# S5 scan with the backward direction in reversed time, its input matrices prepared for all groups, and one step of the cosine on ScalarE

## Chip, cores and metric

One core of a Trainium2 chip runs the whole program. The metric is the device time of one execution in microseconds. The kernel before was run three times: median 1742.31 us, lowest 1741.55, highest 1746.58. In the text, PE is TensorE, DVE VectorE, ACT ScalarE, POOL GpSimd and SP the engine whose queue issues nearly all DMAs. Everything is computed in float32 (some products in a split of it).

## What is computed

The reference is one encoder block on 1024 positions of 1024 channels. The change lies in one of its two token mixers, S5: 512 channels in 32 groups of 16, each group with 64 complex states per direction. Cut to that:

```python
def _s5_scan(u, lam_re, lam_im, log_step, b_re, b_im, c_re, c_im, reverse):
    step = exp(log_step)[:, None]; mag = exp(lam_re * step)
    abar_re, abar_im = mag * cos(lam_im * step), mag * sin(lam_im * step)
    # coef = (abar - 1) / lam, complex
    bb_re = coef_re[..., None] * b_re - coef_im[..., None] * b_im
    bb_im = coef_re[..., None] * b_im + coef_im[..., None] * b_re
    bu_re = einsum('blgc,gpc->lbgp', ug, bb_re); bu_im = einsum('blgc,gpc->lbgp', ug, bb_im)
    # state(t) = abar * state(t-1) + bu(t); from the end where reverse
    s_re, s_im = associative_scan(combine, (a_re, a_im, bu_re, bu_im), reverse=reverse)
    return einsum('lbgp,gcp->blgc', s_re, c_re) - einsum('lbgp,gcp->blgc', s_im, c_im)

y = u * d + _s5_scan(u, ..., reverse=False) + _s5_scan(u, ..., reverse=True)
z = gelu(y); y_a = (z * sigmoid(z @ glu_w + glu_b)) @ w_branch_a
```

The other mixer (Hyena: projections, short convolutions and long convolutions in the frequency domain), the gates, the merge and a SwiGLU feed-forward layer follow.

## The kernel before

The block is emitted stage by stage (hybrid_block, line 1780): norm and Hyena filters, four projections with convolutions, S5 (emit_s5, line 738), eight more projections with convolutions, the gates' projections (emit_gates_a), the GLU on S5's result (emit_glu), Hyena, the merge, the feed-forward layer. A scheduler of the framework sets the order on each engine from the stages' order as written and a model of the engines; on the chip each engine then takes its instructions in that fixed order. So TensorE's projections of the later stages stand between the S5 products, and GpSimd's remainders of the weights (wl, line 136, in the split of a float32 weight into two parts) between its S5 work.

S5 has 128 partitions: 0 to 63 hold the forward direction's 64 states, 64 to 127 the backward direction's (f and b in the code). Time is cut into 128 chunks of 8 steps. s5_params (line 595) computes the per-state coefficients as small [128, 32] arrays, on VectorE; its pool is given back when they are done, and only then are the loop's first loads issued. The loop over q (line 772) takes four of the 32 groups at a time:

- It loads b and c of the four groups (braw, craw), multiplies b by the coefficient on GpSimd (cmul, lines 591 and 592, with tiles bt, giving Bb), and with the powers of abar in a chunk (wt, giving Bw), also on GpSimd.
- c with the powers gives CC on VectorE (lines 797, 798). TensorE transposes c (tc, line 786) and Bw (tt, line 807); ScalarE copies the latter to BT.
- kp (line 819) gives the kernel inside a chunk, which goes through DRAM to a Toeplitz matrix D.
- The phase of each chunk's rotation (lines 839 to 843, ACT and DVE) becomes sine and cosine: three passes on ScalarE (lines 845 to 847: the absolute value and two sines), a square on ScalarE (848), 1 - 2x on VectorE (849), a product on VectorE (850).
- bu, the chunks' inputs to the states, is eight products on TensorE (line 856), 128 x 128 with 128 columns, for real and imaginary parts of four groups. VectorE rotates it (860 to 862) into xs.
- VectorE scans xs over the chunks, once forwards on partitions 0 to 63 and once backwards in the free dimension on 64 to 127, each for the real and the imaginary part (S):

```python
V.tensor_tensor_scan(out=o[f, 1:n], data0=r[f, 0:n - 1], data1=x[f, 0:n - 1], ...)
V.tensor_tensor_scan(out=o[b, n - 2::-1], data0=r[b, n - 1:0:-1], data1=x[b, n - 1:0:-1], ...)
```

- The states are rotated back into M, the real part on VectorE and the imaginary part on GpSimd (875 to 877, tiles rt and beside). TensorE sums C times M over both directions and D times the input in yp (881, 883), 12 products. ScalarE copies yp to z (885), which goes to DRAM (zS).

Tiles with one buffer (z, S, ph, M) and the engines' fixed orders set what can run ahead. In PSUM, bu0, bu1 and yp have a bank each.

Of the kernel before, what the change touches and what calls it, by code (L numbers as in the profile page):

```python
# [7 lines left out]
F32 = mybir.dt.float32  # L8
# [41 lines left out]
def make_constants():  # L50
# [57 lines left out]
    for s_ in range(2):  # L108
# [12 lines left out]
        "c_j8": np.repeat(np.stack([8.0 * np.arange(P), 8.0 * np.arange(P)[::-1]]).astype(np.float32), 64, axis=0),  # L121
# [473 lines left out]
def s5_params(E, op, sp, ps):  # L595
# [136 lines left out]
    keep = op.tile([P, 5, G], F32, name="s5keep")  # L732
    for i, a in enumerate((cre, cim, r8, w, wl)):
        nc.gpsimd.tensor_copy(keep[:, i], a)
    return (keep[:, 0], keep[:, 1]), keep[:, 2], keep[:, 3], keep[:, 4], ec, eb


def emit_s5(E, before):
# [5 lines left out]
    with ExitStack() as ctx:  # L744
# [7 lines left out]
        with E.tc.tile_pool(name="s5p", bufs=1, reuse_waits="tile") as pp:  # L752
            coef, r8, wh, wl, ec, eb = s5_params(E, op, pp, ps)
            before()
# [17 lines left out]
        for q in range(8):  # L772
            gs = slice(4 * q, 4 * q + 4)
            B4 = lambda ap, n: ap[:, gs].unsqueeze(2).to_broadcast([P, 4, n])
            braw = [T(f"braw{i}", [P, 4, 16], 2) for i in range(2)]
            craw = [T(f"craw{i}", [64, P], 2) for i in range(2)]
            for s in range(2):
                r = slice(64 * s, 64 * s + 64)
                for i, n in enumerate(("re", "im")):
                    nc.sync.dma_start(out=braw[i][r], in_=d["s5_b_" + n][0, s, gs].rearrange("g p c -> p g c"))  # L780
# [18 lines left out]
            Bb = [T(f"bb{i}", [P, 4, 16], 2) for i in range(2)]  # L799
            cmul(E, sp, Bb, braw, [B4(coef[0], 16), B4(coef[1], 16)], [P, 4, 16], "bt", GP)  # L800
# [48 lines left out]
            V.tensor_scalar(out=co, in0=co, scalar1=-2.0, scalar2=1.0, op0=ALU.mult, op1=ALU.add)  # L849
# [3 lines left out]
            for i in range(2):  # L853
                pt = ps.tile([P, 4, P], F32, tag=f"bu{i}", name=f"bu{i}")
                for g in range(4):
                    nc.tensor.matmul(out=pt[:, g], lhsT=BT[i][:, g], rhs=U[:, g], start=True, stop=True)
                bu.append(pt)
# [8 lines left out]
            for i in range(2):  # L866
                o, r, x = fl(S[i]), fl(rd), fl(xs[i])
                V.tensor_tensor_scan(out=o[f, 1:n], data0=r[f, 0:n - 1], data1=x[f, 0:n - 1], initial=0.0,
                                     op0=ALU.mult, op1=ALU.add)
                V.tensor_tensor_scan(out=o[b, n - 2::-1], data0=r[b, n - 1:0:-1], data1=x[b, n - 1:0:-1], initial=0.0,  # L870
# [7 lines left out]
            yp = ps.tile([P, 4, P], F32, tag="yp", name="yp")  # L878
            for g in range(4):
                for k in range(2):  # L880
# [1028 lines left out]
```

## Time and profile before

| | |
|---|---|
| median of three runs | 1742.31 us (1741.55 to 1746.58) |
| profiled execution, its own time | 1741.92 us |
| its span | 1740.1 us |
| PE busy | 1548.8 us (89%) |
| PEld (weight loads) busy | 1282.4 us (74%) |
| DVE busy | 1352.2 us (78%) |
| ACT busy | 720.0 us (41%) |
| POOL busy | 674.4 us (39%) |
| S5 loop | about 400 to 634 us of the span |

The span runs from the first to the last instruction of the program; the execution's own time also has what lies around it. The profile's shares are means over stages with different limits, so a stage has to be looked at by itself: its windows, its groups of instructions, its waits. An instruction's names are those of its tiles (out<-in); a matmul in float32 appears as two records.

### The profile page before, as it was taken

The numbers are of one execution on the slowest core, as the hardware profiler recorded it, in microseconds if no ns is written. First come the engines' busy times: TensorE is split into PE (matmuls) and PEld (weight loads), VectorE is DVE, ScalarE is ACT, GpSimd is POOL, SyncE is SP. The second block draws the span as 40 slices with busy tenths as digits, with TensorE's granted clock in tenths as the row PEclk, the third lists the DMA queues.
The fourth block names the chain that finished last, engine by engine and source line by source line (L and its number), as shares of the span: only waits on it lengthen the run. The fifth ranks groups of instructions, "written<-read, shape, count | busy, mean of one in ns | idle before, by whom it ended". The sixth has DMA issues, their size and how long they took to land. (4 is left out here: it accounts for less than half of the span.)

```text
span 1740.1 us, 21907 instructions
## 1 busy us (share of the span) xinstructions
PE 1548.8 (89%) x7470; PEld 1282.4 (74%) x7470; DVE 1352.2 (78%) x1945; ACT 720.0 (41%) x1326; POOL 674.4 (39%) x475
## 2 busy tenths in 40 slices
PE   6777889998777798998869999899999999999996
PEld 2666768776666676786757989688888888878884
DVE  6889798688999935788887666976676777579976
ACT  5846455543333325412223355533333333245445
POOL 3356654329775526768862121111111111011242
PEclk9999999998888899999979999899999999999998
DMA  9446643423232235874326753143323223499963
GB/s 330 122 140 185 194 120 111 154 77 102 64 78 58 76 98 168 292 236 146 120 85 208 258 176 97 49 137 112 103 91 103 91 97 103 147 374 312 331 193 124
DMA packets 245318, 263.81 MB, mean 152 GB/s; under 512 B 28120, under 2 KB 169264, under 8 KB 243765
## 3 DMA queue, kind: packets, MB, share of 16 engines
q1 hardware_dynamic: 244726, 259.99, 47.0%
q0 software_dynamic: 480, 2.42, 0.4%
q8 instruction: 59, 0.97, 0.2%
q14 instruction: 53, 0.43, 0.1%
HBM read 195.00 MB, written 67.34 MB: 151 GB/s over the span
## 5 line engine op out<-in xcount | busy, mean ns | idle before, releaser
L144 PE MATMUL pj<-hT,wh 128*128 128x512 f32 x480 | 196.0, 408 | 10.0 <-ACT cva L1180 8.9
L146 PE MATMUL pj<-hT,wl 128*128 128x512 f32 x480 | 194.5, 405 | 3.5 <-POOL wl L136 3.5
L136 POOL TENSOR_TENSOR wl<-wf,wh 128x1024 fp32r<-128x1024 f32 (+1 forms) x56 | 130.5, 2330 | 157.6 <-ACT wh L135 129.8
L136 POOL TENSOR_TENSOR wl<-wg,wh 128x1024 fp32r<-128x1024 f32 x22 | 54.7, 2488 | 346.9 <-ACT wh L135 346.8
L146 PE MATMUL gu<-h2T,op 128*128 128x512 f32 x440 | 173.1, 394 | 4.3 <-DVE op L136 4.3
L144 PE MATMUL gu<-h2T,op 128*128 128x512 f32 x440 | 171.4, 394 | 2.6 <-ACT op L135 2.5
L145 PE MATMUL gu<-h2T,op 128*128 128x512 f32 x440 | 172.7, 392 | 0.0
L135 ACT CAST op<-ws 128x512 fp32r<-128x512 f32 x88 | 54.4, 621 | 181.3 <-PE gu L146 109.4
L145 PE MATMUL dn<-dop 128*128 128x512 f32 x308 | 120.1, 390 | 0.4 <-POOL dop L136 0.4
L146 PE MATMUL dn<-dop 128*128 128x512 f32 x308 | 119.9, 389 | 0.0
L144 PEld LDWEIGHTS pj<-hT,wh 128*128 128x128 f32 x480 | 94.5, 197 | 29.5 <-ACT cva L1180 9.6
L144 PE MATMUL dn<-dop 128*128 128x512 f32 x308 | 112.4, 390 | 2.9 <-ACT dop L135 2.9
L146 PEld LDWEIGHTS pj<-hT,wl 128*128 128x128 f32 x480 | 93.9, 196 | 23.1 <-POOL wl L136 4.3
L145 PE MATMUL pj<-hT,wh 128*128 128x512 f32 x256 | 104.6, 409 | 0.0
L146 PEld LDWEIGHTS gu<-h2T,op 128*128 128x128 f32 x440 | 83.6, 190 | 22.7 <-DVE op L136 5.2
L144 PEld LDWEIGHTS gu<-h2T,op 128*128 128x128 f32 x440 | 83.7, 190 | 21.3 <-ACT op L135 3.4
L145 PEld LDWEIGHTS gu<-h2T,op 128*128 128x128 f32 x440 | 83.7, 190 | 17.2
L145 PE MATMUL pj<-lT,wh 128*128 128x512 f32 x224 | 89.8, 401 | 0.0
L136 POOL TENSOR_TENSOR dop<-bf,dop 128x512 fp32r<-128x512 f32 x17 | 32.2, 1897 | 128.8 <-ACT dop L135 112.5
L1531 DVE TENSOR_TENSOR ws<-wu 128x512 f32<-128x512 f32 x22 | 24.9, 1130 | 66.2 <-DMA wu<-in_ffn_w_gu_dram 66.2
L144 PE MATMUL wop<-woh,mT 128*128 128x256 f32 x256 | 73.1, 286 | 2.3 <-DVE tmp L1406 2.1
L145 PE MATMUL wop<-wol,mT 128*128 128x256 f32 x256 | 72.5, 283 | 0.0
(458 smaller groups left out, 4503.5 us busy)
## 6 DMA issues: line engine op xcount, KB each, us to landing
bf<-in_ffn_w_down_dram SPq DMA_DIRECT2D x105, 256.0 KB
wf<-in_w_in_dram SPq DMA_DIRECT2D x36, 512.0 KB
ada<-in_ada_w_dram SPq DMA_DIRECT2D x48, 256.0 KB
wg<-in_ffn_w_gu_dram SPq DMA_DIRECT2D x22, 512.0 KB
wu<-in_ffn_w_gu_dram SPq DMA_DIRECT2D x22, 512.0 KB
adS<-S SPq DMA_DIRECT2D x44, 256.0 KB
af<-adS SPq DMA_DIRECT2D x44, 256.0 KB
adA<-a SPq DMA_DIRECT2D x33, 256.0 KB
```

What stands on the lines that cost most here:

```text
L135: E.nc.scalar.copy(hi, src)
L136: (lo_eng or E.nc.vector).tensor_tensor(out=lo, in0=src, in1=bc(hi), op=ALU.subtract)
L144: E.nc.tensor.matmul(out=out, lhsT=lh, rhs=rh, start=first, stop=False, skip_group_check=shared)
L145: E.nc.tensor.matmul(out=out, lhsT=lh, rhs=rl, start=False, stop=False, skip_group_check=shared)
L146: E.nc.tensor.matmul(out=out, lhsT=ll, rhs=rh, start=False, stop=last, skip_group_check=shared)
L1531: V.tensor_tensor(out=s1, in0=u1, in1=u2, op=ALU.add)
```

## The change

s5_params now loads all of b (four DMAs), computes Bb for all 32 groups on VectorE in six instructions, and keeps it; the loop takes slices of it. The backward direction's states are held in reversed time: bu's half for the backward direction is made from the input with its columns reversed, so that both directions scan forwards in one instruction of 128 partitions; c_j8, the chunk numbers for the phase, is then the same in both halves. For y, the backward half of M is read with its columns reversed into a PSUM tile of its own, yb, which shares two buffers with bu0 and bu1; ScalarE copies yb to z, and VectorE adds yp to it. The cosine's 1 - 2x is a pass on ScalarE.

```diff
@@ -118,7 +118,7 @@
         "c_dft_lo": lo.astype(np.float32),
         "c_tab": tab.astype(np.float32),
         "c_feat": feats,
-        "c_j8": np.repeat(np.stack([8.0 * np.arange(P), 8.0 * np.arange(P)[::-1]]).astype(np.float32), 64, axis=0),
+        "c_j8": np.repeat(8.0 * np.arange(P, dtype=np.float32)[None], P, axis=0),
     }
 
 
@@ -729,10 +729,16 @@
         nc.scalar.copy(ebt[i][f], pw[i][f, 7::-1])
         nc.scalar.copy(ebt[i][b], pw[i][b, 0:8])
     cmul(E, sp, eb, ebt, [x.unsqueeze(1).to_broadcast([P, 8, G]) for x in u8], [P, 8, G], "ebm", conj=True)
-    keep = op.tile([P, 5, G], F32, name="s5keep")
-    for i, a in enumerate((cre, cim, r8, w, wl)):
+    Bb = [op.tile([P, G, 16], F32, name=f"bb{i}") for i in range(2)]
+    raw = [sp.tile([P, G, 16], F32, name=f"braw{i}") for i in range(2)]
+    for x, n in zip(raw, ("re", "im")):
+        for s in range(2):
+            nc.sync.dma_start(out=x[64 * s:64 * s + 64], in_=d["s5_b_" + n][0, s].rearrange("g p c -> p g c"))
+    cmul(E, sp, Bb, raw, [x.unsqueeze(2).to_broadcast([P, G, 16]) for x in (cre, cim)], [P, G, 16], "bt")
+    keep = op.tile([P, 3, G], F32, name="s5keep")
+    for i, a in enumerate((r8, w, wl)):
         nc.gpsimd.tensor_copy(keep[:, i], a)
-    return (keep[:, 0], keep[:, 1]), keep[:, 2], keep[:, 3], keep[:, 4], ec, eb
+    return Bb, keep[:, 0], keep[:, 1], keep[:, 2], ec, eb
 
 
 def emit_s5(E, before):
@@ -750,7 +756,7 @@
         j8 = op.tile([P, 1, P], F32, name="j8")
         nc.sync.dma_start(out=j8[:, 0], in_=d["c_j8"])
         with E.tc.tile_pool(name="s5p", bufs=1, reuse_waits="tile") as pp:
-            coef, r8, wh, wl, ec, eb = s5_params(E, op, pp, ps)
+            bball, r8, wh, wl, ec, eb = s5_params(E, op, pp, ps)
             before()
         sp = ctx.enter_context(E.tc.tile_pool(name="s5", bufs=1, reuse_waits="tile"))
         halfpi = op.tile([P, 1], F32, name="halfpi")
@@ -771,13 +777,10 @@
         beside = E.dft.tile([P, 4, 4, P], F32, tag="ax", name="beside")
         for q in range(8):
             gs = slice(4 * q, 4 * q + 4)
-            B4 = lambda ap, n: ap[:, gs].unsqueeze(2).to_broadcast([P, 4, n])
-            braw = [T(f"braw{i}", [P, 4, 16], 2) for i in range(2)]
-            craw = [T(f"craw{i}", [64, P], 2) for i in range(2)]
+            craw = [T(f"craw{i}", [64, P]) for i in range(2)]
             for s in range(2):
                 r = slice(64 * s, 64 * s + 64)
                 for i, n in enumerate(("re", "im")):
-                    nc.sync.dma_start(out=braw[i][r], in_=d["s5_b_" + n][0, s, gs].rearrange("g p c -> p g c"))
                     nc.sync.dma_start(out=craw[i][:, r], in_=d["s5_c_" + n][0, s, gs].rearrange("g c p -> (g c) p"))
             e4 = lambda ap, n, m: ap[:, :, gs].rearrange("p t g -> p g t").unsqueeze(3).to_broadcast([P, 4, n, m])
             b4 = lambda ap, n, m: ap.unsqueeze(2).to_broadcast([P, 4, n, m])
@@ -796,8 +799,7 @@
                 for i in range(2):
                     V.tensor_tensor(out=tmp[i], in0=b4(cv(c_, i), 9, 16), in1=e4(ec[i ^ k], 9, 16), op=ALU.mult)
                 V.tensor_tensor(out=CC[k], in0=tmp[0], in1=tmp[1], op=sgn)
-            Bb = [T(f"bb{i}", [P, 4, 16], 2) for i in range(2)]
-            cmul(E, sp, Bb, braw, [B4(coef[0], 16), B4(coef[1], 16)], [P, 4, 16], "bt", GP)
+            Bb = [x[:, gs] for x in bball]
             Bw = [T(f"bw{i}", [P, 4, 8, 16]) for i in range(2)]
             cmul(E, sp, Bw, [b4(x, 8, 16) for x in Bb], [e4(x, 8, 16) for x in eb], [P, 4, 8, 16], "wt", GP)
             BT = []
@@ -846,14 +848,15 @@
             nc.scalar.activation(out=ph, in_=ph, func=ACTF.Sin, scale=float(np.pi))
             nc.scalar.activation(out=kk, in_=kk, func=ACTF.Sin, scale=-float(np.pi), bias=halfpi)
             nc.scalar.activation(out=co, in_=ph, func=ACTF.Square)
-            V.tensor_scalar(out=co, in0=co, scalar1=-2.0, scalar2=1.0, op0=ALU.mult, op1=ALU.add)
+            nc.scalar.activation(out=co, in_=co, func=ACTF.Identity, scale=-2.0, bias=1.0)
             V.scalar_tensor_tensor(out=si, in0=ph, scalar=2.0, in1=kk, op0=ALU.mult, op1=ALU.mult)
             nc.scalar.copy(rd[:, :, 1:P + 1], J(r8))
             bu = []
             for i in range(2):
-                pt = ps.tile([P, 4, P], F32, tag=f"bu{i}", name=f"bu{i}")
+                pt = ps.tile([P, 4, P], F32, tag="bu", name=f"bu{i}", bufs=2)
                 for g in range(4):
-                    nc.tensor.matmul(out=pt[:, g], lhsT=BT[i][:, g], rhs=U[:, g], start=True, stop=True)
+                    for r, x in ((f, U[:, g]), (b, U[:, g, ::-1])):
+                        nc.tensor.matmul(out=pt[r, g], lhsT=BT[i][:, g, r], rhs=x, start=True, stop=True)
                 bu.append(pt)
             for i, sgn in ((0, ALU.add), (1, ALU.subtract)):
                 p = [T(f"rt{k}") for k in range(2)]
@@ -865,9 +868,7 @@
             n = 4 * W
             for i in range(2):
                 o, r, x = fl(S[i]), fl(rd), fl(xs[i])
-                V.tensor_tensor_scan(out=o[f, 1:n], data0=r[f, 0:n - 1], data1=x[f, 0:n - 1], initial=0.0,
-                                     op0=ALU.mult, op1=ALU.add)
-                V.tensor_tensor_scan(out=o[b, n - 2::-1], data0=r[b, n - 1:0:-1], data1=x[b, n - 1:0:-1], initial=0.0,
+                V.tensor_tensor_scan(out=o[:, 1:n], data0=r[:, 0:n - 1], data1=x[:, 0:n - 1], initial=0.0,
                                      op0=ALU.mult, op1=ALU.add)
             M = [T(f"M{i}") for i in range(2)]
             for i, sgn, eng in ((0, ALU.subtract, V), (1, ALU.add, GP)):
@@ -876,13 +877,17 @@
                 eng.tensor_tensor(out=p[1], in0=S[1][:, :, 1:P + 1], in1=(si, co)[i], op=ALU.mult)
                 eng.tensor_tensor(out=M[i], in0=p[0], in1=p[1], op=sgn)
             yp = ps.tile([P, 4, P], F32, tag="yp", name="yp")
+            yb = ps.tile([P, 4, P], F32, tag="bu", name="yb", bufs=2)
             for g in range(4):
+                w = [x[:, g, 1:9].rearrange("p i c -> p (i c)") for x in CC]
                 for k in range(2):
-                    nc.tensor.matmul(out=yp[:, g], lhsT=CC[k][:, g, 1:9].rearrange("p i c -> p (i c)"), rhs=M[k][:, g],
-                                     start=k == 0, stop=False)
-                nc.tensor.matmul(out=yp[:, g], lhsT=D[:, g], rhs=U[:, g], start=False, stop=True)
+                    nc.tensor.matmul(out=yb[:, g], lhsT=w[k][b], rhs=M[k][b, g, ::-1], start=k == 0, stop=k == 1)
+                nc.tensor.matmul(out=yp[:, g], lhsT=D[:, g], rhs=U[:, g], start=True, stop=False)
+                for k in range(2):
+                    nc.tensor.matmul(out=yp[:, g], lhsT=w[k][f], rhs=M[k][f, g], start=False, stop=k == 1)
             z = T("z")
-            nc.scalar.copy(z, yp)
+            nc.scalar.copy(z, yb)
+            V.tensor_tensor(out=z, in0=yp, in1=z, op=ALU.add)
             nc.sync.dma_start(out=E.zS[q // 2][4 * (q % 2):4 * (q % 2) + 4].rearrange("g t c j -> (t c) g j"), in_=z)
```

The order on the engines moves with it. VectorE, first, from the phase of the group after next (line 843 before, 845 now) to the scans of the next group (the order's name for a scan is SCALAR_TENSOR_TENSOR). Before:

```order
L843 SCALAR_TENSOR_TENSOR ph<-j_2291,s5keep,ph 128x128 x4
L860 TENSOR_TENSOR rt_3827<-bu_3817,cos 128x512
L861 TENSOR_TENSOR rt_3828<-bu_3822,sin 128x512
L862 TENSOR_TENSOR xs_2816<-rt_3827,rt_3828 128x4x128
L860 TENSOR_TENSOR rt_3832<-bu_3822,cos 128x512
L861 TENSOR_TENSOR rt_3833<-bu_3817,sin 128x512
L868 SCALAR_TENSOR_TENSOR S_3837<-rd,xs_2816 64x519
L870 SCALAR_TENSOR_TENSOR S_3837<-rd,xs_2816 64x519
L862 TENSOR_TENSOR xs_2817<-rt_3832,rt_3833 128x4x128
```

Now:

```order
L845 SCALAR_TENSOR_TENSOR ph<-j_2291,s5keep,ph 128x128 x4
L890 TENSOR_TENSOR z<-yp,z 128x512
L863 TENSOR_TENSOR rt_3823<-bu_3805,cos 128x512
L827 SCALAR_TENSOR_TENSOR kb<-diag,dcol,kb 64x16
L828 TENSOR_TENSOR Kt<-kp,kb 64x16
L864 TENSOR_TENSOR rt_3824<-bu_3814,sin 128x512
L865 TENSOR_TENSOR xs_2832<-rt_3823,rt_3824 128x4x128
L863 TENSOR_TENSOR rt_3828<-bu_3814,cos 128x512
L864 TENSOR_TENSOR rt_3829<-bu_3805,sin 128x512
L871 SCALAR_TENSOR_TENSOR S_3833<-rd,xs_2832 128x519
L865 TENSOR_TENSOR xs_2833<-rt_3828,rt_3829 128x4x128
L871 SCALAR_TENSOR_TENSOR S_3834<-rd,xs_2833 128x519
```

The addition for z (line 890) stands between the phase and the rotation of the next group, and the scans are two instead of four. In six of the eight groups z's addition follows the phase, or the phase and one product.

ScalarE, from the phase's scaling to the copies behind z. Before:

```order
L839 ACTIVATE ph<-j_2291,s5keep 128x128 x4
L1233 ACTIVATE ga<-pj 128x512
L809 COPY BT_3407<-tt 128x512
L809 COPY BT_3414<-tt 128x512
L845 ACTIVATE phk<-ph 128x512
L846 ACTIVATE ph<-ph 128x512
L847 ACTIVATE phk<-phk,halfpi 128x512
L885 COPY z<-yp 128x512
L815 COPY bz_2814<-bb_3552 64x4x16 x2
L823 COPY Kt<-kp 128x144
```

Now:

```order
L841 ACTIVATE ph<-j_2291,s5keep 128x128 x4
L135 CAST wh<-wf 128x1024
L1238 ACTIVATE ga<-pj 128x512
L847 ACTIVATE phk<-ph 128x512
L848 ACTIVATE ph<-ph 128x512
L849 ACTIVATE phk<-phk,halfpi 128x512
L889 COPY z<-yb 128x512
L817 COPY bz_2830<-bb_2511 64x4x16 x2
L825 COPY Kt<-kp 128x144
```

The three passes over the phase (lines 847 to 849 now, 845 to 847 before) stood ahead of z's copy before as well; z's copy now has yb as its source and is followed by VectorE's addition.

TensorE, the last of a group's four parts and the start of the kernel inside the chunk. Before:

```order
L881 MATMUL yp<-M_2973,cc_2844 128x128
L881 MATMUL yp<-M_2974,cc_2845 128x128
L883 MATMUL yp<-U,D 128x128
L819 MATMUL kp<-cc_3019,bz_2815 128x144
L819 MATMUL kp<-cc_3018,bz_2814 128x144
```

Now:

```order
L884 MATMUL yb<-M_3321,cc_3198 128x128
L884 MATMUL yb<-M_3322,cc_3199 128x128
L885 MATMUL yp<-U,D 128x128
L887 MATMUL yp<-M_3321,cc_3198 128x128
L887 MATMUL yp<-M_3322,cc_3199 128x128
L821 MATMUL kp<-cc_3370,bz_2830 128x144
L821 MATMUL kp<-cc_3371,bz_2831 128x144
```

A part has five products in place of three: two of half the rows into yb, D times the input over all rows, and two of half the rows into yp. bu's products (line 859 now) are 64 rows of output each, eight for a real or imaginary part.

## Rows read from the trace of the kernel before

**Rows 1.** Windows view around the S5 loop (columns in its first line)

```profile
core 0: us, PE busy (x) PEld busy (x) DVE busy (x) ACT busy (x) POOL busy (x), PEclk, DMA share, GB/s
...
520.00:560.00 40.00, 29.10 (x139) 24.46 (x140) 39.70 (x42) 10.91 (x27) 28.00 (x19) 0.81 0.17 49
...
640.00:680.00 40.00, 36.19 (x151) 28.93 (x150) 10.93 (x6) 21.89 (x23) 13.99 (x6) 0.96 0.64 180
```

**Rows 2.** Windows view, the S5 loop as one stretch

```profile
400.00:634.00 234.00, 180.88 (x919) 151.22 (x918) 214.96 (x218) 71.34 (x165) 159.55 (x116) 0.87 0.27 74
```

**Rows 3.** Line 877 on VectorE: ns min/median/max, first and last start

```profile
L877 DVE TENSOR_TENSOR M<-rt,rt x8: 692/1530/1635, 429.3 to 627.2; 128x512 f32<-128x512 f32 x8
```

**Rows 4.** Groups of VectorE, 400 to 634 us: busy us, mean ns

```profile
L870 DVE TENSOR_TENSOR_SCAN S<-rd,xs 64x519 f32<-64x519 f32 x16 | 27.6, 1723 | 0.2
...
L868 DVE TENSOR_TENSOR_SCAN S<-rd,xs 64x519 f32<-64x519 f32 x16 | 23.1, 1443 | 0.1
...
L877 DVE TENSOR_TENSOR M<-rt,rt 128x512 f32<-128x512 f32 x8 | 11.5, 1436 | 0.5
...
L860 DVE TENSOR_TENSOR rt<-bu,cos 128x512 f32<-128x512 f32 x16 | 11.0, 686 | 4.7 <-PE bu L856 4.4
...
L849 DVE TENSOR_SCALAR cos<-cos 128x512 f32<-128x512 f32 x7 | 6.0, 859 | 0.0
```

**Rows 5.** Groups of GpSimd, 400 to 634 us

```profile
L591 POOL TENSOR_TENSOR bt<-braw,s5keep 128x64 f32<-128x64 f32 x26 | 17.2, 681 | 0.4
...
L592 POOL TENSOR_TENSOR bb<-bt,bt 128x64 f32<-128x64 f32 x14 | 10.1, 719 | 11.5 <-ACT bz L815 11.4
```

**Rows 6.** Groups of VectorE by shape, whole span

```profile
L250 DVE TENSOR_TENSOR fbt<-f,ex 128x512 f32<-128x512 f32 x32 | 21.7, 677 | 1.5 <-ACT ex L247 1.5
...
L972 DVE TENSOR_TENSOR acc<-acc,aw 1x512 f32<-1x512 f32 x2 | 1.4, 676 | 0.0
```

**Rows 7.** Instructions of line 797 on VectorE

```profile
L797 DVE TENSOR_TENSOR rt<-ct,ec x16: 746/1660/2956, 399.9 to 604.4; 128x576 f32<-128x576 f32 x16
```

**Rows 8.** Timeline of ScalarE: start us, us, instruction

```profile
399.99 0.63 ACT L845 ACTIVATE phk<-ph 128x512 f32<-128x512 f32 x1 [3.35 <-DVE ph L843]
400.65 0.63 ACT L846 ACTIVATE ph<-ph 128x512 f32<-128x512 f32 x1
401.19 0.71 ACT L847 ACTIVATE phk<-phk,halfpi 128x512 f32<-128x512 f32 x1
401.80 0.57 ACT L809 COPY BT<-tt 128x512 f32<-128x512 f32 x1
```

**Rows 9.** Waits, 390 to 640 us: total, times, longest us

```profile
ACT phk L845 <- DVE ph L843: 51.3, 7, 10.6
...
PE yp L881 <- DVE M L877: 20.3, 8, 6.8
```

**Rows 10.** Timeline of TensorE, 631 to 639 us

```profile
631.78 0.39 PE L883 MATMUL yp<-U,D 128*128 128x128 f32 x2
...
632.45 0.39 PE L883 MATMUL yp<-U,D 128*128 128x128 f32 x2
...
635.63 0.39 PE L144 MATMUL pj<-hT,wh 128*128 128x512 f32 x1
...
638.37 0.39 PE L144 MATMUL pj<-hT,wh 128*128 128x512 f32 x1
```

**Rows 11.** Timeline of TensorE, 15 to 20 us

```profile
15.84 2.07 PE L191 MATMUL hps<-sin_h,w 128*128 128x512 f32 x2 [4.26 <-ACT sin_h L168]
17.84 1.97 PE L188 MATMUL hps<-feat,w 33*64 33x512 f32 x4
```

**Rows 12.** Timeline of all engines, 467 to 469 us

```profile
467.96 0.27 PE L786 MATMUL tc<-ident,craw 64*128 64x64 f32 x1
...
468.16 0.49 PE L883 MATMUL yp<-U,D 128*128 128x128 f32 x2
...
468.49 0.61 PE L881 MATMUL yp<-M,cc 128*128 128x128 f32 x4
```

## The prediction

> **What bounds the kernel now.** I read the windows view first, since the diff touches one stage alone. The reader is to see in it that the S5 loop is VectorE's: 39.70 of 40 us busy, TensorE 29.10 at a granted clock of 0.81, while right after the loop TensorE has 36.19 of 40 at 0.96 and VectorE 10.93 [rows 1]. Over the whole loop, from 400 to 634 us, VectorE works 214.96 of 234 us, GpSimd 159.55 [rows 2]. The period comes from the first and last start of the product M on VectorE: (627.2 - 429.3) / 7 = 28.3 us for a group of four [rows 3]. The waits say the same: in the loop TensorE stands for M, 20.3 us in 8 times, and ScalarE for the phase [rows 9]. So a microsecond off VectorE's row of work is worth a microsecond per group, until another engine or a new wait takes over. After the loop TensorE has a fixed rest of projections to do, so that an earlier end of the loop shifts the rest of the kernel with it.
>
> **The scans.** A group has two scans on line 868 and two on line 870, 64 partitions each, with means of 1443 and 1723 ns: 2 x 1.443 + 2 x 1.723 = 6.33 us [rows 4]. Afterwards there are two, with 128 partitions. No row shows a scan of 128; that an instruction's time does not go with its partitions is seen at an addition of 512 elements, 677 ns on 128 partitions and 676 on one [rows 6]. I take the mean of the two means, 1.58 us: 3.17 saved per group (bounds 2.9 and 3.4).
>
> **The cosine's step and the addition for z.** Line 849 costs VectorE 859 ns [rows 4] and goes to ScalarE, which works 71.34 of 234 us [rows 2] and pays some 0.63, like its other passes over that size [rows 8]. New on VectorE is z = yp + z, one operand from PSUM, as line 860 has it: 0.69 us [rows 4].
>
> **Input matrices.** GpSimd loses 26 and 14 small instructions in the stretch, 17.2 + 10.1 = 27.3 us [rows 5], 17% of its 159.55. It is not the bound itself, but VectorE is slower beside it: line 877 has a mean of 1436 ns [rows 4] and a minimum of 692 [rows 3], line 797 a median of 1660 and a minimum of 746 [rows 7]. Take scans (6.3) and the four PSUM-fed products (2.7) from 28.3 and some 19 us are of this kind; up to half of it, 9 us, is then waiting for GpSimd, and 17% of that is 1.5 us per group. Since the removed instructions are short I take 0.7, with bounds of 0 and 1.5. For it, six instructions of 512 elements come once on VectorE ahead of the loop, 6 x 0.69 = 4.1 us (at most 6 x 1.5 = 9); four loads, issued right behind those of the parameters, replace 32 in the loop, so that SP's queue has 28 issues less. The small arithmetic that GpSimd did before the first group leaves the way of that group, but two of GpSimd's weight remainders (wl) now stand ahead of its first product there, so I let the first group's input come about 1 us later (bounds 8 earlier, 4 later).
>
> Per group, VectorE then does 28.3 - 3.17 - 0.86 + 0.69 - 0.7 = 24.3 us.
>
> **A new wait.** The addition for z stands on VectorE right behind the phase for the group after next (line 843 before) and ahead of the next group's products. It needs the copy of yb on ScalarE, and that copy stands behind three passes over the same phase, which can start only when VectorE has finished it; ScalarE already waits for that phase 7 times [rows 9]. The three passes take from 399.99 to 401.80, 1.81 us, and a copy from PSUM 0.57 [rows 8]. So VectorE stands for 1.81 + 0.57 and a handover, 2.5 us, before it can add; queued behind are the products, both scans and with them M. It happens in six groups: the last two have no phase to come. Bounds: 1.8, if GpSimd's part of the contention is worked off meanwhile, and 3.3, if a gate's activation of 0.6 us slips in between. Of the old program no row shows this wait, since there VectorE never read z. The same copy frees the PSUM buffer of the next group's second bu, for yb now shares two buffers with both bu: eight half products, 0.9 us in pairs, come behind it, and VectorE has the addition and a product, 2 x 0.69 us, to do meanwhile, so that this costs nothing; if the pairs do not share their time, 1.8 us, it is 0.4 per group.
>
> **TensorE.** A 128x128 product of 128 columns takes (632.45 - 631.78) / 3 = 0.223 us, a projection's (638.37 - 635.63) / 12 = 0.228 [rows 10]. bu goes from 8 products of full width to 16 of half. The two halves lie in different columns of the array, and there is a case of that in the trace: line 188's four records take 1.97 us where two records of the same length and full width take 2.07 [rows 11]. I count a pair as one, at 0.223 (bound: two). y goes from 12 products to 20, +1.8 us. Going in and out of a product of half the rows has a price too: the transpose of craw, 64 columns, keeps the next product off for 0.20 us where 0.06 were its own, and the two records behind it take 0.33 instead of 0.22 [rows 12], so about 0.125 for a change of shape. In the new order there are 16 of these per group, instead of 3: 2.0 us. A group is then 49 x 0.228 + (8 + 8 + 20) x 0.223 + 8 x 0.25 for kp + 0.4 for the transposes + 2.0 = 23.6 us at the full clock; 25.4 if the pairs of bu do not share their time. Both lie under the 26.5 that VectorE needs with its wait, so I count this work at nothing in the loop; its cover is those 26.5 us, of which TensorE would fill nine tenths.
> The Trainium skill, TensorEngine Tiling (Array Packing), Key Properties, speaks against this part: a change of tiling mode drains the engine. By that rule the 16 changes have a price, and the trace agrees, with its 0.125 us; were they free, TensorE would have 21.6 us per group and the sum would stay as it is, VectorE being longer either way.
>
> **The sum.** Seven periods: 7 x (28.3 - 24.3) = 28.0 saved, six waits of 2.5 = 15.0 back. The first group: two scans less, one microsecond later, -2.0. The end of the last group: eight products more, 1.8, and the addition, 0.7: +2.5. Behind the loop 140 projection products are left instead of 148: -1.8. Together -28.0 + 15.0 - 2.0 + 2.5 - 1.8 = -14.3 us. The profiled execution took 1741.92 us (span 1740.1); that gives **1727.6**. The median of the three runs, 1742.31, lies 0.4 above it.
>
> **Rivals.** No change is what lies within 0.3%, 5.2 us.
> *The wait does not bite* (0.20): yb's copy is done before VectorE comes to it. For it speaks that ScalarE is under a third busy; against it, that the three passes stand ahead in a fixed order and themselves need VectorE. Then 15 us are not given back: 1712.6, and with all of GpSimd's relief (0.8 x 7) 1707.
> *TensorE takes part of it* (0.08): 25.4 us of work at a clock of 0.93 are 27.3 per group, 7 x 1.0 saved and the ends' -1.3: 1734.
> *It comes out even* (0.10): the same at 0.90, 28.2 per group: 1740.
> *TensorE becomes the bound and it is slower* (0.07): the clock stays where it was in the loop. At 0.87 [rows 2] 25.4 us of work are 29.2, +0.9 x 7 - 1.3: 1747; at the 0.81 of the stretch from 520 to 560 [rows 1] they are 31.4: 1762. It decides from 25.4 / 28.3 = 0.90 granted downwards. Against it: the low clock comes in stretches in which TensorE stands for M, and that standing gets shorter.
> *The change does not do what it says* (0.03): a scan of 128 partitions takes as long as both halves. VectorE then keeps 28.3 + 0.69 - 0.86 - 0.7 = 27.4 and gets the wait: about 29.5, 1749. [rows 6] speak against it.
>
> **How the numbers follow.** The forecast, VectorE with its new wait, has 0.52; its own range goes from 1718 (waits of 1.8 and all relief, -4.2 and -5.6) to 1737 (waits of 3.3 and no relief, +4.8 and +4.9). Faster by over 0.3% are this one, the first rival and the second: 0.80; the same 0.10; slower 0.10. The range of 8 in 10 takes in the forecast's own, most of the first rival and the second: 1708 to 1739; it leaves out that rival's low end and both slower cases.
>
> **What would show it.** In the new trace: the scans 16 in number with 1.2 to 1.7 us each; line 890 on VectorE with some 2.5 us of idle time ahead of it, ended by ScalarE's copy, in six groups; M's starts some 26.5 us apart; the halves of bu starting in pairs; TensorE's clock in the loop above 0.87. Scans of over 2.5 us, or M's starts further apart than 28 us with TensorE busy throughout, would make the forecast wrong; starts 24 us apart with no idle time ahead of line 890 too.

## The result, and the profile after

The changed kernel takes **1770.3 us** (median; 1768.53 to 1772.64), the kernel before 1742.28 in the same comparison: a ratio of 1.0156, 95% interval 1.0136 to 1.0177. It is 28 us slower, where 1727.6 was forecast and the range ended at 1739. The profiled execution took 1768.53 us, its span is 1766.8.

First the stage. The windows view of the changed kernel over its loop, and over one stretch of 13 us in it (columns as in [rows 1]):

```profile
400.00:660.00 260.00, 213.11 (x1157) 169.98 (x1155) 195.40 (x209) 81.86 (x184) 128.04 (x74) 0.80 0.22 62
...
541.00:554.00 13.00, 13.00 (x56) 10.22 (x56) 4.85 (x11) 3.57 (x9) 0.00 (x0) 0.50 0.28 82
```

VectorE, 214.96 of 234 us busy before [rows 2], now has 195.40 of 260: it waits. TensorE's granted clock fell from 0.87 to 0.80. In the 13 us below, TensorE is busy throughout at half the clock, and VectorE has 4.85 us of work. The period, from line 878 in place of 877 [rows 3]:

```profile
L878 DVE TENSOR_TENSOR M<-rt,rt x8: 1481/1641/1667, 435.8 to 657.6; 128x512 f32<-128x512 f32 x8
```

(657.6 - 435.8) / 7 = 31.7 us, against 28.3. The first product of the GLU starts at 701.2 us instead of 673.7. The first M is 6.5 us later, the seven periods are 23.9 longer, from the last M to the GLU it takes 43.6 us instead of 46.5 (-2.9), and the rest is 0.8 shorter: +26.7, the difference of the spans.

What VectorE waits for, by its groups of instructions from 395 to 670 us:

```profile
L871 DVE TENSOR_TENSOR_SCAN S<-rd,xs 128x519 f32<-128x519 f32 x16 | 27.9, 1746 | 1.5 <-DVE xs L865 0.9
...
L863 DVE TENSOR_TENSOR rt<-bu,cos 128x512 f32<-128x512 f32 x16 | 11.0, 690 | 13.8 <-PE bu L859 13.5
L864 DVE TENSOR_TENSOR rt<-bu,sin 128x512 f32<-128x512 f32 x16 | 10.9, 684 | 8.9 <-PE bu L859 8.9
...
L890 DVE TENSOR_TENSOR z<-yp,z 128x512 f32<-128x512 f32 x8 | 5.5, 691 | 27.2 <-issue 13.0 <-PE yp L887 9.3 <-ACT z L889 4.9
...
L827 DVE SCALAR_TENSOR_TENSOR kb<-diag,dcol,kb 64x16 f32<-64x16 f32 x8 | 1.8, 220 | 12.4 <-ACT kb L826 12.4
```

The scans do what was said: 16 in place of 32, 27.9 us in place of 50.7 [rows 4]. But 27.2 us of idle time stand ahead of the addition for z (21.8 of them in the six groups that were forecast), 22.7 ahead of bu's rotation (lines 863, 864), and 12.4 ahead of the small addition to kp (5.7 of them before the first M). In the seven periods VectorE is busy for 167.3 us, 23.9 per group, and stands for 54.5; before, it stood for 8.2 of 197.9.

One group shows why. TensorE's timeline from 533 to 556 us (start, us, instruction; what it stood for in brackets):

```profile
533.28 0.34 PE L884 MATMUL yb<-M,cc 64*128 64x128 f32 x1 [1.68 <-DVE M L878]
...
533.70 0.88 PE L859 MATMUL bu<-U,BT 128*64 128x128 f32 x12
540.92 0.82 PE L821 MATMUL kp<-cc,bz 128*128 128x144 f32 x2 [6.34 <-DVE cc L801]
...
542.88 1.06 PE L884 MATMUL yb<-M,cc 64*128 64x128 f32 x4
...
548.74 0.84 PE L887 MATMUL yp<-M,cc 64*128 64x128 f32 x3
549.51 3.73 PE L821 MATMUL kp<-cc,bz 128*128 128x144 f32 x14
553.17 0.69 PE L859 MATMUL bu<-U,BT 128*64 128x128 f32 x2
...
555.88 1.09 PE L859 MATMUL bu<-U,BT 128*64 128x128 f32 x16
```

And VectorE in the same stretch:

```profile
543.95 1.14 DVE L845 SCALAR_TENSOR_TENSOR ph<-j,s5keep,ph 128x128 f32<-128x128 f32 x4
549.68 0.69 DVE L890 TENSOR_TENSOR z<-yp,z 128x512 f32<-128x512 f32 x1 [4.59 <-issue]
553.90 0.69 DVE L863 TENSOR_TENSOR rt<-bu,cos 128x512 f32<-128x512 f32 x1 [3.53 <-PE bu L859]
...
557.02 0.69 DVE L864 TENSOR_TENSOR rt<-bu,sin 128x512 f32<-128x512 f32 x1 [2.10 <-PE bu L859]
```

M is ready at 533, and the first pieces of y run. Then TensorE's queue has kp's first product for the next group, and that needs cc, which VectorE makes only after M: TensorE stands for 6.34 us, and all that is left of y stands behind it. When it goes on, its granted clock is 0.50, the lower of its two levels (1.2 GHz of 2.4): a piece of y, or a pair of pieces of yp and yb, every 0.21 us, where the same pieces at 511 us, at full clock, start 0.11 us apart. y ends at 549.6, and the addition starts right then (the "issue" of its bracket is a wait the records don't name; the times do). The last bu comes behind y, yb's copy and kp, at 555.88. ScalarE's copy, which the forecast had as the last to come, started at 547.77, before y's end.

It is not so in every group. M starts at 435.8, 469.4, 505.1, 531.5, 568.3, 603.9, 634.3 and 657.6 us. In the third and in the last period, 26.4 and 23.3 us long, kp's first product stands behind y in TensorE's queue; in the other five, 30.4 to 36.8 us long, it stands ahead of most of y. The third period and the one after it, and the third's y, kp and addition:

```profile
505.09:531.49 26.40, 23.91 (x147) 19.11 (x147) 23.54 (x27) 10.38 (x25) 17.25 (x11) 0.94 0.24 63
531.49:568.26 36.77, 28.74 (x148) 22.59 (x147) 26.15 (x27) 10.47 (x25) 17.69 (x11) 0.72 0.22 63
...
513.31 0.71 PE L887 MATMUL yp<-M,cc 64*128 64x128 f32 x4
513.94 0.51 PE L821 MATMUL kp<-cc,bz 128*128 128x144 f32 x2
...
519.11 0.69 DVE L890 TENSOR_TENSOR z<-yp,z 128x512 f32<-128x512 f32 x1 [2.44 <-ACT z L889]
```

The third period goes as it was forecast: 26.4 us, 2.44 us ahead of the addition, ended by ScalarE's copy, no wait for bu, TensorE busy for 23.9 us.

Before, kp's first product stood ahead of most of y as well, but nothing on VectorE waited for y there, and bu seldom: 5.7 us in the seven periods, in the two groups whose last bu product stood behind y and kp.

### The profile page after: what moved, and what is told of

The parts are those of the page before. It is cut to its first block, busy times and chain, and to the rows that moved or that the text cites. A ratio compares the mean times of both kernels' runs of the same rounds, so it can differ in the third digit from the quotient of the medians.

```text
span 1766.8 us, 22293 instructions
## 1 busy us (share of the span) xinstructions
PE 1583.6 (90%) x7726; PEld 1301.6 (74%) x7726; DVE 1330.2 (75%) x1935; ACT 725.5 (41%) x1334; POOL 646.7 (37%) x425
## 5 line engine op out<-in xcount | busy, mean ns | idle before, releaser
L144 PE MATMUL pj<-hT,wh 128*128 128x512 f32 x480 | 192.1, 400 | 9.4 <-ACT cva L1185 8.7
L145 PE MATMUL pj<-hT,wh 128*128 128x512 f32 x256 | 101.1, 395 | 0.0
L146 PEld LDWEIGHTS gu<-h2T,op 128*128 128x128 f32 x440 | 83.5, 190 | 22.4 <-DVE op L136 5.0
```

Source lines behind the costliest of these rows:

```text
L144: E.nc.tensor.matmul(out=out, lhsT=lh, rhs=rh, start=first, stop=False, skip_group_check=shared)
L145: E.nc.tensor.matmul(out=out, lhsT=lh, rhs=rl, start=False, stop=False, skip_group_check=shared)
L146: E.nc.tensor.matmul(out=out, lhsT=ll, rhs=rh, start=False, stop=last, skip_group_check=shared)
```

## The experiments

Each run is compared with the kernel before on the same chip; its median there lay between 1739.6 and 1743.8 us, so that a difference between two runs taken on different chips can be off by up to 4 us. In brackets stand the ratio to the kernel before and its 95% interval. With every edit the scheduler makes a new order for all engines, so that no run differs from another by its edit alone. Of longer edits the diffs show the main lines.

**1. M's backward half in natural time, 12 products for y, no addition, a bank for each bu.**

```diff
-                eng.tensor_tensor(out=M[i], in0=p[0], in1=p[1], op=sgn)
+                eng.tensor_tensor(out=M[i][f], in0=p[0][f], in1=p[1][f], op=sgn)
+                eng.tensor_tensor(out=M[i][b], in0=p[0][b, :, ::-1], in1=p[1][b, :, ::-1], op=sgn)
```

> The changed kernel, but M's backward half is written in natural time by an instruction of its own (64 partitions, columns reversed), so that y is 12 products into yp as before, ScalarE copies yp to z, VectorE adds nothing, and bu0 and bu1 have a PSUM bank each again. One instruction more per group on VectorE and on GpSimd. Theory A (VectorE's row of work is tied to the y products of the group before, by the shared PSUM buffers and by the addition for z; in the changed kernel it stood 21.8 us ahead of line 890 in six groups and 28 us more for bu): these stalls go, M starts 25 to 26 us apart, time 1725 to 1738. Theory B (TensorE's own work at a low clock is the bound, the stalls only show it): bu still has 64 half-width pieces per group of eight, M starts stay over 29 us apart, time over 1752.

1750.4 us (1.0045, 1.0029 to 1.0060): 20 us back. M starts 27.8 us apart. That lies between the two theories: y's new way was the larger part of the loss, but a shorter period did not become time one for one.

**2. yb ahead of yp in the same bank; the two bu have theirs again.**

```diff
-            yb = ps.tile([P, 4, P], F32, tag="bu", name="yb", bufs=2)
+            yb = ps.tile([P, 4, P], F32, tag="yp", name="yb")
```

> The changed kernel, but yb takes yp's PSUM bank, ahead of yp and one after the other, and bu0 and bu1 have their own banks again: bu no longer waits for yb's copy. The addition for z stays on VectorE. Theory A1 (the shared PSUM buffer is the main price: rotation waits for bu, bu for yb's copy, that for y): the idle time ahead of lines 863, 864 and 827, 28 us, falls under 8, and the time to 1742 to 1752. Theory A2 (VectorE's addition standing in front of the rotation is the main price): the idle time stays ahead of that addition and the time above 1762.

1759.3 us (1.0085, 1.0066 to 1.0104), between the two theories. VectorE's groups, 400 to 640 us:

```profile
L864 DVE TENSOR_TENSOR rt<-bu,sin 128x512 f32<-128x512 f32 x16 | 10.9, 679 | 0.4 <-PE bu L859 0.3
L892 DVE TENSOR_TENSOR z<-yp,z 128x512 f32<-128x512 f32 x7 | 4.8, 685 | 18.6 <-PE yp L890 18.6
```

The wait for bu is gone with the shared buffer, the one for yp has stayed. The period fell from 31.7 us to 28.0; of the 25.7 us in seven groups only 11 came out as time.

**3. The addition for z on GpSimd** (ScalarE copies yp as well).

```diff
-            V.tensor_tensor(out=z, in0=yp, in1=z, op=ALU.add)
+            z2 = beside[:, 2 * (q % 2)]
+            nc.scalar.copy(z2, yp)
+            GP.tensor_tensor(out=z, in0=z2, in1=z, op=ALU.add)
```

> The changed kernel, but the addition for z is on GpSimd: ScalarE copies yp too, into a buffer in SBUF, and GpSimd adds it. VectorE never waits for yp. The shared PSUM buffers stay. Theory A1 (the shared buffer alone ties the rotation to y): the stall moves from the addition to the rotation's products, the time stays at 1763 to 1773. Theory A2 (the addition is the price): 21.8 us of stall and 0.69 us of work in eight groups go, 1742 to 1750.

1770.3 us (1.0153), no change. VectorE's groups, 400 to 665 us:

```profile
L863 DVE TENSOR_TENSOR rt<-bu,cos 128x512 f32<-128x512 f32 x16 | 11.0, 690 | 17.2 <-PE bu L859 16.8
...
L827 DVE SCALAR_TENSOR_TENSOR kb<-diag,dcol,kb 64x16 f32<-64x16 f32 x8 | 4.2, 521 | 42.0 <-ACT kb L826 42.0
```

The stall moved to bu and to kb. bu and kp stand behind y on TensorE as well; and ScalarE's copy of kp for kb now stands behind its new copy of yp, so that part of the 42.0 us can be this edit's own. That taking the addition off VectorE changed nothing shows that the addition alone was not the price: the lateness is there without it.

**4. The cosine's step back on VectorE**, in the changed kernel.

> The changed kernel with the cosine's step, 1 - 2x, back on VectorE (0.5 to 0.9 us per group); all else as changed. If VectorE's work still sets the period: slower by 4 to 7 us, 1774 to 1777. If the period is a round of waits through TensorE and the step falls into a stall: within 3 us of 1770.

1778.1 us (1.0192, 1.0174 to 1.0210), 7.8 slower.

**7. That step alone on ScalarE**, in the kernel before:

```diff
-            V.tensor_scalar(out=co, in0=co, scalar1=-2.0, scalar2=1.0, op0=ALU.mult, op1=ALU.add)
+            nc.scalar.activation(out=co, in_=co, func=ACTF.Identity, scale=-2.0, bias=1.0)
```

> The kernel before with only the cosine's step on ScalarE. If VectorE's row of work sets the period, as the prediction has it: 0.86 us less in eight groups, 1735 to 1738. If the time goes by TensorE's queue (its work, its slow stretches and its idle time up to the first GLU product, together 282.9 us before and 309.7 in the changed kernel) and a shorter row on VectorE only leaves more projections for behind the loop: within 3 us of before.

1737.5 us (0.9965, 0.9954 to 0.9976), 5.5 faster. VectorE's work between M and cc counts in both kernels; this part of the forecast was right.

**5, 6, 8. The input matrices.** Run 5 gives the changed kernel the old ones back (GpSimd, group by group), run 6 gives the kernel before the new ones alone, run 8 is run 1 with the old ones.

> The changed kernel with the input matrices made as before: b loaded four groups at a time and multiplied on GpSimd in six small instructions per group. If VectorE's six instructions ahead of the loop are what made it start late (the first M began at 435.8 us instead of 429.3): 5 to 7 us faster than the changed kernel, 1763 to 1766. If GpSimd's relief was worth the 0.7 us per group that the prediction gave it: 5 us slower, 1775.

> The kernel before with only the input matrices for all groups at once on VectorE; scans, bu, y and cosine as before. If the late start is the price and nothing comes back: 1747 to 1750. If GpSimd's relief pays for it (0.7 us in seven periods): within 2 us of before.

> The kernel of the first experiment (M's backward half written in natural time, 12 products for y, a bank for each bu) with the input matrices on GpSimd as before. What stays of the change: one scan for both directions, bu in halves, the cosine's step on ScalarE. If the late start was what kept the first experiment 6.6 us above the kernel before: 1743 to 1746. If bu's halves were (128 products more, 5.7 us more of TensorE's time in the changed kernel): 1749 to 1752.

Run 5: 1753.0 us (1.0057, 1.0037 to 1.0076), 17 less than the changed kernel. Run 6: 1751.3 (1.0044, 1.0029 to 1.0060), 8.3 more than before. Run 8: **1734.1** (0.9949, 0.9934 to 0.9963), 16 less than run 1, and faster than both kernels. The part that was priced as the smallest brought the largest miss. In runs 5 and 8 the first M is 10.1 and 9.0 us earlier than in their twins. In run 6, from the first M to the last and from there to the GLU, the windows view of TensorE's projections alone (busy time and count of PE, PEld and ACT, then clock and DMA; the count is what is read here):

```profile
436.90:629.60 192.70, 90.70 (x306) 64.10 (x306) 7.64 (x13) 0.84 0.22 63
629.60:679.40 49.80, 42.44 (x182) 33.88 (x182) 4.15 (x7) 1.00 0.52 146
```

and before:

```profile
429.30:627.20 197.90, 93.47 (x331) 66.82 (x331) 8.28 (x14) 0.86 0.26 70
627.20:673.70 46.50, 38.48 (x158) 30.34 (x158) 3.54 (x6) 0.96 0.48 127
```

The loop starts 7.6 us later. GpSimd's relief is real: 192.7 us for seven periods, not 197.9, or 0.74 per group. But the order has 306 projections in the loop instead of 331, and 182 behind instead of 158: 3.3 us are given back.

**9, 15. Where they are made.** Run 9 is run 1 with them made ahead of the loop by GpSimd, run 15 is run 8 with them made in the loop by VectorE.

> The kernel of the first experiment (1750.4 us) with the input matrices still made for all groups at once ahead of the loop, but by GpSimd's six instructions instead of VectorE's. Theory: what is dear in that part is its place on VectorE ahead of the last coefficients, which starts the loop 8 us later; GpSimd stood idle there. Then the first M starts at 426 to 429 us and the time is 1730 to 1736, level with or below the 1734.1 of the eighth run. Rival: its price is not the place but what a lighter GpSimd does to the order in the loop; then the time stays at 1746 or more.

> The kernel of the eighth run (1734.1 us) with the input matrices still made group by group in the loop, but on VectorE: six instructions of 64 elements per group there instead of on GpSimd. If GpSimd's lighter load is what costs in the changed kernel (by another order): 1742 or more. If only the place ahead of the loop costs: VectorE pays some 0.7 us per group and gets about as much back from GpSimd, 1731 to 1738.

1765.0 us (1.0125, 1.0106 to 1.0145) and 1748.5 (1.0038, 1.0026 to 1.0051): in both the place ahead of the loop fails as the explanation, and the other theory's time came, that a GpSimd with less to do in the loop costs through another order. Every kernel here that takes this work off GpSimd in the loop is slower than its twin that leaves it there, by 8 to 31 us in six pairs. What in the order does it is not shown. In run 15 the first M starts at 428.5 us, against 426.4 in run 8, and the periods are shorter (27.2 and 27.5 us), and yet it is 14 us slower. Run 15, last M to GLU (projections alone):

```profile
618.80:675.60 56.80, 48.26 (x203) 38.50 (x201) 4.84 (x8) 0.97 0.44 128
```

In run 8 there are 46.7 us in that place, with 188 projections. At 0.228 us each [rows 10] the 15 more are some 3.4 of the 10.1 us; for 6.1 us of the 56.8 TensorE stands, against 1.0 of the 46.7. Why the order comes out so was not tried and stays open.

**10. Run 8 with the cosine's step on VectorE**: of the change, the single scan alone.

> The kernel of the eighth run (1734.1 us) with the cosine's step back on VectorE: of the change only the single scan, with bu in halves and M written in natural time, is left. If the parts add: the step was worth 5.5 us alone, so 1739 to 1741. If the single scan is worth nothing by itself: 1742 or more.

1740.3 us (0.9982, 0.9972 to 0.9993). The parts add here: 6.2 us between runs 10 and 8, and the single scan with what it needs is worth 2, not the 22 (7 x 3.17) that the sum had for it.

**11, 12. The new y alone, and bu in halves alone**, in the kernel before. Run 11's edit is the change's for y without the reversed columns; run 12's:

```diff
-                    nc.tensor.matmul(out=pt[:, g], lhsT=BT[i][:, g], rhs=U[:, g], start=True, stop=True)
+                    for r in (f, b):
+                        nc.tensor.matmul(out=pt[r, g], lhsT=BT[i][:, g, r], rhs=U[:, g], start=True, stop=True)
```

> The kernel before with only the new way for y: 20 products, yb in a PSUM buffer shared with both bu, ScalarE's copy of yb and VectorE's addition; scans in both directions, bu at full width, nothing reversed. If this part is the price (17 to 20 us in the pairs of runs that differ in it): 1758 to 1764, TensorE's slow stretches longer and VectorE idle ahead of the addition and of bu. If it only costs together with the shorter row on VectorE, which leaves nothing to cover it: 1742 to 1750.

> The kernel before with only bu in half-width products, two for each of the old ones, both from the input in natural time. TensorE's occupancy by bu was 18.1 us before and 23.8 in the changed kernel. If TensorE's queue sets the time, and the pairs overlap: 2 to 6 us slower, 1745 to 1749. If bu is hidden: within 2 us of before.

1771.1 us (1.0167, 1.0135 to 1.0199) and 1758.4 (1.0084, 1.0063 to 1.0105), both over what was expected. y's new way costs 28 us by itself (24 to 35), as much as the whole change, and at an unchanged clock in the loop (0.87 in the seven periods, 0.86 before). Here the addition's wait is ended by ScalarE's copy each time, as the forecast had it, but is longer than its 2.5 us; run 11's waits from 400 to 660 us:

```profile
DVE z L889 <- ACT z L888: 22.2, 6, 6.9
```

bu in halves costs 16, far over the price of its pieces. Run 12's waits over the same stretch, and TensorE around one kp:

```profile
DVE rt L862 <- PE bu L857: 14.5, 3, 8.6
PE yp L882 <- POOL M L878: 14.0, 3, 7.0
DVE rt L861 <- PE bu L857: 9.4, 2, 4.9
```

```profile
524.48 1.14 PE L857 MATMUL bu<-U,BT 128*64 128x128 f32 x12
...
528.99 0.39 PE L884 MATMUL yp<-U,D 128*128 128x128 f32 x2
531.78 3.64 PE L819 MATMUL kp<-cc,bz 128*128 128x144 f32 x14 [2.40 <-DVE cc L798]
535.35 0.88 PE L857 MATMUL bu<-U,BT 128*64 128x128 f32 x12
```

The last pieces of bu stand behind y and kp in the queue. They take about a microsecond; what counts is their place. In other groups they stand behind a product of y that waits for GpSimd's part of M, a wait that the kernel before did not have. VectorE's rotation stands for bu for 24 us in the loop, against 10.8 before. Up to the GLU this is 8.5 us of the 16; where the rest arises behind it is not shown.

**13, 14, 16. kp behind y.** kp's PSUM tile takes yp's bank, so that its products follow y's in TensorE's queue, in the changed kernel, in the one before, and in that of run 8.

```diff
-            kp = ps.tile([P, 9, 16], F32, tag="tt", name="kp", bufs=2)
+            kp = ps.tile([P, 9, 16], F32, tag="yp", name="kp")
```

> The changed kernel with kp's PSUM tile in yp's bank, so that kp's products stand behind the y products of the group before in TensorE's queue and no longer ahead of them. Theory Q (y is late because it stands behind kp's first product, which waits for the next group's cc on VectorE): y follows M at once, the idle time of VectorE ahead of line 890 falls from 21.8 us to under 8, time 1750 to 1760. Theory W (the y products themselves, 54.0 us of TensorE's time against 27.2, set it): the idle time only moves, over 1765.

> The same edit in the kernel before, as a control: nothing on VectorE waits for y there. Theory Q: within 4 us of before, 1739 to 1747, since y's lateness costs only TensorE's idle time, which moves from one place to the other. If the shared bank itself costs something (kp must wait for yp's copy): slower by 5 us or more.

> The kernel of the eighth run with kp's tile in yp's bank. Nothing on VectorE waits for y there, but bu's products for the next group can stand behind y and kp. Theory Q: TensorE's idle time ahead of kp (21.9 us) shrinks, 1726 to 1733. If it only moves to y or to bu: 1732 to 1740.

1760.9 us (1.0105, 1.0082 to 1.0128), 1736.4 (0.9975, 0.9962 to 0.9987) and **1728.7** (0.9923, 0.9898 to 0.9947). The edit is worth 9.4, 4.6 and 5.4 us. The control, run 14, was to stay level and did not: so not all of run 13's 9.4 us comes from VectorE's wait for y. Run 13's waits and its loop's window:

```profile
DVE kb L827 <- ACT kb L826: 20.1, 5, 5.5
...
DVE z L890 <- ACT z L889: 13.5, 6, 2.4
DVE rt L864 <- PE bu L859: 10.2, 4, 4.0
...
PE bu L859 <- ACT z L889: 9.4, 4, 3.8
...
PE kp L821 <- DVE cc L801: 7.0, 1, 7.0
```

```profile
400.00:660.00 260.00, 226.22 (x1334) 179.36 (x1333) 200.01 (x210) 89.21 (x196) 133.25 (x79) 0.95 0.26 78
```

TensorE's wait for cc is down from 34.5 us to 7.0, and its clock in the loop is up from 0.80 to 0.95. And now the addition waits for ScalarE's copy in all six groups, 13.5 us where 15.0 were forecast: that wait is what remains once the greater one is gone. But M still starts 30.0 us apart, (647.1 - 437.3) / 7, and not 26.5. VectorE stands for bu and kb as well, and TensorE itself stands for ScalarE's copy before it can begin bu: that is the shared buffer. Part of the wait for kb is this edit's own, for kp's tile is free only when the addition has read yp. And the GLU begins at 668.7 us, 32 us earlier than in the changed kernel, while the kernel is only 9.4 us faster: where the GLU begins does not tell the time by itself, for the order behind the loop is another one too.

**17, 18. Two sums.** Run 17 is the kernel before with the cosine's step on ScalarE and kp behind y; run 18 the changed kernel with the old input matrices and kp behind y.

> The kernel before with the cosine's step on ScalarE and kp's tile in yp's bank; scans, bu and y as before. If the single scan with what it needs is worth the 3.4 us that lie between the seventh and the eighth run: some 3 to 5 us over the 1728.7 of the sixteenth run, 1731 to 1735. If it is worth nothing then: 1727 to 1730.

> The changed kernel with the input matrices on GpSimd as before (17.4 us faster alone) and kp's tile in yp's bank (9.4 us faster alone). If the two prices are separate: 1742 to 1746, level with before. If both cure the same waiting: 1749 to 1754.

1728.4 us (0.9938, 0.9926 to 0.9951) and 1749.3 (1.0046, 1.0031 to 1.0062). Run 17 has none of the reversed time and is level with run 16, within the intervals of the two: with kp behind y no worth of the single scan was measured. In run 18 the two cures overlap, and it stays 8 us slower than the kernel before, although its GLU begins at 659.2 us, 14 us earlier than there.

## Why the prediction was wrong

Of the 41 us between the forecast and the profiled execution (1727.6 and 1768.53), 37 lie in the seven periods, forecast 13.0 us shorter and measured 23.9 longer. Another 8.5 lie in the start of the first M, forecast 2.0 earlier and measured 6.5 later; 4.4 came back behind the last M.

- **"What bounds the kernel now"**: VectorE's row of work was forecast well, 24.3 us per group against 23.9 measured, and work added to it or taken from it counts (runs 4 and 7). But "an earlier end of the loop shifts the rest of the kernel with it" fails: the rest is not fixed. Run 6 shortened seven periods by 5.2 us and paid 3.3 behind the loop; runs 1 and 2 brought the period under the old one and stayed slower; in run 15 the last M starts at 618.8 us, 8.4 earlier than before, and the kernel is slower by 7.
- **The scans and the cosine** were nearly right in size: two scans of 1.746 us per group where 1.58 were taken, a saving of 2.84 us, just under the lower bound of 2.9; and 5.5 us for the step where seven periods of 0.86, 6.0 us, were in the sum.
- **The input matrices**: the relief was sized well (0.7 us per group, 0.74 in run 6), the late start was not (1 us later in the sum, bound 4; 7.6 in run 6). Giving the old way back brings 16 to 17 us in two pairs of runs, 9 to 10 of them at the start of the first M; the cause of the rest stays open.
- **"A new wait", the step that failed.** Its place was right, in six groups, its size was not: VectorE's idle time in the seven periods was 54.5 us, where the forecast had 15.0 on top of the 8.2 of before. The wait was priced from ScalarE's copy alone, at 2.5 us. In two of the six groups it was that, 2.44 us, ended by the copy; in the four others it was 3.8 to 4.6, set by yp, which stood behind kp's first product. That product's place was in the order that the forecast had at hand, and kp's wait for cc, 21.1 us in 12 times, was in the trace of the kernel before: it was not looked up who stands behind it.
- **"So that this costs nothing"**, in the same step, of the shared PSUM buffer, is the larger error: bu was taken to come right behind yb's copy. It came behind y and kp too, and VectorE stood for bu for 22.4 us in the seven periods (5.7 before). Run 2, with the bank no longer shared, took that wait away and brought the period from 31.7 to 28.0 us; run 13, with kp out of the way, brought it to 30.0.
- **"I count this work at nothing in the loop"**: 23.6 us per group at full clock were to fit under VectorE's 26.5. The size was right: in the third period, with kp behind y, TensorE was busy for 23.9 us, at a clock of 0.94. The cover was wrong: in five of seven periods the products came in a block, behind a wait, at half clock, and VectorE waited for the last of them. TensorE's groups, 400 to 660 us after (without the last group's y), then 400 to 634 before:

```profile
L821 PE MATMUL kp<-cc,bz 128*128 128x144 f32 x128 | 31.3, 414 | 34.5 <-DVE cc L801 34.5
L887 PE MATMUL yp<-M,cc 64*128 64x128 f32 x112 | 31.0, 409 | 0.0
...
L884 PE MATMUL yb<-M,cc 64*128 64x128 f32 x112 | 28.8, 402 | 10.2 <-DVE M L878 10.2
L859 PE MATMUL bu<-U,BT 128*64 128x128 f32 x256 | 25.2, 313 | 0.2 <-ACT z L889 0.2
```

```profile
L881 PE MATMUL yp<-M,cc 128*128 128x128 f32 x128 | 26.0, 323 | 20.3 <-DVE M L877 20.3
...
L819 PE MATMUL kp<-cc,bz 128*128 128x144 f32 x128 | 22.6, 325 | 21.1 <-DVE cc L798 21.1
L856 PE MATMUL bu<-U,BT 128*128 128x128 f32 x128 | 21.2, 312 | 0.2 <-ACT BT L809 0.2
```

kp is the same 128 records in both and went from 325 to 414 ns: the clock. From the start of the loop (390.8 us before, 391.5 after) to the first GLU product TensorE stands idle 283 - 226 = 57 us before and 310 - 257 = 53 after; what grew is its busy time, by 31 us. The clock is not the whole of it: in run 13 it is 0.95 in the loop and the kernel is still slower than before, and in run 11 it did not fall. The rival that came nearest, "TensorE becomes the bound", was given 0.07 and 1747 to 1762. The argument against it, that TensorE's standing would get shorter and its clock rise, failed in its second half: the standing got shorter by 4 us, the clock fell, and the standing came to lie just ahead of the work that VectorE waits for.

## What to carry to other kernels

Before a wait is priced, follow the releaser back through its own queue: the price is that of the last thing ahead of it there, and an early product that waits for the waiting engine closes a circle. A buffer shared between a consumer's input and its own late result does the same without showing in any duration. Where a backlog of other work stands behind the loop, do not count a shorter loop as time saved one for one. And look at the periods one by one: here one of seven went as forecast, and what differed in it pointed to the cause.

## What was not expected of the hardware

After standing 6.34 us, TensorE was busy for 13 us without a gap at a granted clock of 0.50, its lower level of 1.2 GHz (the window of 541 to 554 us above), through y's pieces, kp and bu; from 555 us on it was at 1.00. With kp behind y the clock in the loop was 0.95.

The halves of bu share their time: at full clock 16 records of half the columns take 1.09 us after (at 555.88 us, above), and 8 of full width take 1.06 before, so that a pair takes hardly longer than one product of full width. The halves of y do so too, where a piece of yp and one of yb stand next to each other in the queue: they start 0.01 us apart. First bu before, then two pieces of y after:

```profile
548.56 1.06 PE L856 MATMUL bu<-U,BT 128*128 128x128 f32 x8
...
545.18 0.42 PE L887 MATMUL yp<-M,cc 64*128 64x128 f32 x1
545.19 0.42 PE L884 MATMUL yb<-M,cc 64*128 64x128 f32 x1
```

And a scan of 128 partitions takes 1746 ns, as long as one of 64 (1723 for the backward one [rows 4]).
